# Layer 0's residual and norm steps held in PSUM, and convolution work moved from VectorE to GpSimd, in a two-layer hybrid trunk

## The chip, the cores and the metric

The kernel runs on one core of one Trainium2 chip. The engines of a core work in parallel, each through its own queue in order: TensorE (PE, with its weight loads as PEld), VectorE (DVE), ScalarE (ACT), GpSimd (POOL) and SyncE (SP), which issues all of this kernel's transfers. The metric is the device time of one execution in microseconds, as a median over runs.

## The reference

The input `x` is 512 rows of 1024 float32 numbers. Two layers each compute `x <- x + RMSNorm_post(mixer(RMSNorm_pre(x)))`.

```python
def rms_norm(x, g):
    return x * lax.rsqrt(jnp.mean(x * x, axis=-1, keepdims=True) + EPS) * g

for i in range(DEPTH):
    h = rms_norm(x, pre_norm_g[i])
    y = even_mixer(h, ...) if i % 2 == 0 else odd_mixer(h, ...)
    x = x + rms_norm(y, post_norm_g[i])
```

Layer 0's mixer is block-sparse attention beside a causal pooling mixer, layer 1's is an S5 state-space layer beside a Conformer convolution module. What the change touches of layer 1 is the convolution with its layer norm, and the gate of the state-space branch:

```python
def conformer_conv(a, gl, dw, ln_g, ln_b, pw):
    g = a * jax.nn.sigmoid(gl)
    c = causal_depthwise_conv(g, dw)            # 31 taps per channel
    mu = jnp.mean(c, axis=-1, keepdims=True)
    var = jnp.mean(jnp.square(c - mu), axis=-1, keepdims=True)
    n = (c - mu) * lax.rsqrt(var + EPS) * ln_g + ln_b
    return jax.nn.silu(n) @ pw

ya, yb = jnp.split(y @ glu_w + glu_b, 2, axis=-1)
ssm_out = ya * jax.nn.sigmoid(yb) * jax.nn.silu(gc)
```

## The kernel before

All products are done three times over on halves of the operands: a float32 number is split into a rounded high part and the rest (`split`, L108, and the weight splits in `prefetch`, L158), and `mm3` (L102) adds high by high, high by low and low by high into one PSUM bank. ScalarE writes the high part of a weight block (`whi`), and GpSimd (in layer 0's input projections VectorE) subtracts it from the loaded `raw` to get `wlo`. `prefetch` works up to three blocks ahead of TensorE.

The kernel is written in a tile framework. Tiles are taken from pools with a fixed number of buffers for each tag, and a new tile waits for the last reader of the old one in its buffer. The order of the instructions in each engine's queue is not that of the text: a scheduler lays it out before the run, by the place of the instruction in the text (its priority) and by when a simulated timeline has its inputs ready. `issue_after` forces instructions behind a given one on its engine. The queue is fixed once the kernel is built: an engine whose next instruction waits does nothing else.

Layer 0's end (L927 to L956). There are four row blocks t of 128 rows, each with two halves q of 512 columns. For each (t, q), `out_mm` forms the output projection in a PSUM bank `z`; banks come from the pool `pz` (four banks) except that the first halves of t=0 and t=1 live in `ps` (two banks). ScalarE takes the sum of squares (`sumsq`, L309), VectorE multiplies by the gain into an SBUF tile `yg` (a `wt`). When both halves are there, `add_norm` (L912) takes the root (`root2`, `root`: one ScalarE square root and small VectorE steps on 128x1 numbers, L92 to L100), forms the residual sum in `xt` by two wide `scalar_tensor_tensor`s, takes its sums of squares and root, and forms the next layer's normed input `xn` by two more. `next_hT` (L903) transposes `xn` of the block before on TensorE and splits it into `hh` and `hl`. Layer 1's first projection, `sa`, starts with the columns of t=0 and t=1 (L954), in four banks of `pz`, while the last blocks are still being normed; in the same stretch GpSimd splits `sa`'s weights.

The convolution (L1076 to L1124). There are four channel blocks m. `conv_in` (L1078) forms the gated input `gp[m]` when its projection is done: block 0 out of `sa`, 1 out of `sb`, 2 and 3 out of `ab1`. Each tap is one VectorE `scalar_tensor_tensor` on 128x512, which adds into `acc` in PSUM (one bank). The last `NP[m]` taps of a block are done elsewhere (`ptap`, L1092): ScalarE scales the shifted input into `lt`, and GpSimd adds it to `pacc` (two buffers). VectorE adds `pacc` to `acc` right after its first tap, and its last tap writes the sum `ca[m]` to SBUF. `conv` is called after each of the 16 weight blocks of `sb`, `ab1`, `gd` and `gc`, for eight VectorE taps and three others each time.

After the taps, `ln_mean` (L1126) adds the first three `ca`, and TensorE sums over the channels by two matmuls with `ones`, one on that sum (L1131) and one on `ca[3]` (L1132). `ln_var` and `ln_out` follow. The gate of the state-space branch comes from two projections `gl0` and `gl1` of four banks each (L1232 to L1243), which share the four banks of `pz`; `gl1` is forced behind the second mean matmul (`issue_after(ln["mu"])`, L1234). For each half, ScalarE takes a sigmoid, and two VectorE steps form `ct` (L1241, L1242) before it is split.

Of the kernel before, what the change touches and what calls it, by code (L numbers as in the profile page):

```python
# [14 lines left out]
F32 = mybir.dt.float32  # L15
# [3 lines left out]
AF = mybir.ActivationFunctionType  # L19
# [4 lines left out]
MUL, ADD, SUB, MAX, MIN = ALU.mult, ALU.add, ALU.subtract, ALU.max, ALU.min  # L24

T, D = 512, 1024
# [12 lines left out]
def tile_hybrid_trunk(ctx, tc, A):  # L39
# [17 lines left out]
    def tt(e, o, a, b, op):  # L57
        return e.tensor_tensor(o, a, b, op=op)  # L58

    def stt(e, o, a, s, b, op0, op1):  # L60
        e.scalar_tensor_tensor(o, a, s, b, op0=op0, op1=op1)  # L61
# [30 lines left out]
    def root(v, bias, n=1):  # L92

        q, w, r = (sm.tile([128, n], F32, tag=f"{a}{n}", name=a) for a in ("rq", "rw", "rr"))
        S.activation(q, v, AF.Sqrt, bias=bias)
        ts(V, w, v, bias, -0.5, ADD, MUL)
        V.reciprocal(r, q)
        stt(V, q, r, w, r, MUL, MUL)
        stt(V, r, q, 1.5, r, ADD, MUL)
        return r  # L100

    def mm3(p, sh, sl, mh, ml, start, stop):  # L102
# [206 lines left out]
    def sumsq(src, jpool):  # L309
        ss = sm.tile([128, 1], F32, tag="ss", name="ss")  # L310
        jk = jpool.tile([128, 512], BF16, tag="junk", name="junk", bufs=1)
        S.activation(jk[:, 0:src.shape[-1]], src, AF.Square, scale=1.0 / 32.0, accum_out=ss)  # L312
        return ss
# [16 lines left out]
    def wt():  # L330
        return wk.tile([128, 512], F32, tag="t", name="wt", bufs=5)
# [580 lines left out]
    def add_norm(t, yg, ss):  # L912

        r = root2(ss)
        ss = []
        for q in range(2):
            stt(V, xt[t][q], yg[q], r, xt[t][q], MUL, ADD)
            ss.append(sumsq(xt[t][q], wk))
        r = root2(ss)
        if t == 3:  # L920
            S.activation(warm, r, AF.Sigmoid)
        xn = [wt(), wt()]
        for q in range(2):
            stt(V, xn[q], xt[t][q], r, gpre1[q], MUL, MUL)
        return xn

    xns, yg, ss = [], defaultdict(list), defaultdict(list)  # L927
# [8 lines left out]
    for t, q in ((0, 0), (1, 0), (0, 1), (1, 1), (2, 0), (2, 1), (3, 0), (3, 1)):  # L936
        if t < 2 and not q:
            z = z2[t]
        else:
            z = pz.tile([128, 512], F32, tag="z", name="z")  # L940
            out_mm(z, f"o0{q}", full, t, ch, cl, OK0, lambda j: 3 - j)
        ss[t].append(sumsq(z, wk))
        yg[t].append(wt())
        tt(V, yg[t][q], z, gpost[q], MUL)
        if (t, q) == (3, 0):
            prefetch(index["sa", 0] + 4)
        if q:
            if t:
                next_hT(t - 1, xns[t - 1])
            xns.append(add_norm(t, yg[t], ss[t]))  # L950
# [133 lines left out]

    NP = (0, 0, 4, 12)
    taps = [(m, k) for m in range(4) for k in range(KC - NP[m])]
    ptaps = [(m, k) for m in range(4) for k in range(KC - NP[m], KC)]
    acc, pacc = {}, {}  # L1090
# [12 lines left out]
    def conv(n, n_p=3):  # L1103
        for _ in range(n_p):
            if ptaps and gp[ptaps[0][0]] is not None:
                ptap()
        for _ in range(min(n, len(taps))):
            m, k = taps[0]
            if gp[m] is None:
                return  # L1110
            taps.pop(0)
            src, c = gp[m][:, k:k + T], dw[:, m, k:k + 1]
            if k == 0:
                while any(i == m for i, _ in ptaps):
                    ptap()
                acc[m] = pa.tile([128, T], F32, tag="acc", name="acc")
                ts(V, acc[m], src, c, None, MUL)
                if NP[m]:
                    tt(V, acc[m], acc[m], pacc[m], ADD)
                continue  # L1120
            o = acc[m]
            if k == KC - NP[m] - 1:
                o = ca[m] = kp.tile([128, T], F32, tag="ca", name="ca", bufs=4)
            stt(V, o, src, c, acc[m], MUL, ADD)  # L1124

    def ln_mean():  # L1126
        s = lt()
        tt(V, s, ca[0], ca[1], ADD)
        tt(V, s, s, ca[2], ADD)
        mu = ps.tile([128, 512], F32, tag="s", name="mu")  # L1130
        nc.tensor.matmul(mu, ones, s, start=True, stop=False)  # L1131
        ln["mu"] = nc.tensor.matmul(mu, ones, ca[3], start=False, stop=True).ins  # L1132
        for m in range(4):
            tt(V, ca[m], ca[m], mu, SUB)

        def sq(m):
            q = lt()
            S.activation(q, ca[m], AF.Square)
            return q
        a, b, c, ln["q"] = (sq(m) for m in range(4))  # L1140
        tt(V, a, a, b, ADD)
        tt(V, a, a, c, ADD)
        ln["s"] = a
# [88 lines left out]
    for n in range(2):  # L1232

        with tc.issue_after(ln["mu"]) if n else nullcontext():  # L1234
            z = proj_c(f"gl{n}", yh, yl, nk=4)
        for i in range(2):
            m = 2 * n + i
            s = ct()
            S.activation(s, z[2 + i], AF.Sigmoid, bias=gb[:, 4 + m:5 + m])
            a = ct()  # L1240
            stt(V, a, z[i], gb[:, m:m + 1], s, ADD, MUL)  # L1241
            tt(V, a, a, sgc[:, m], MUL)  # L1242
            split(c1[0][:, m], c1[1][:, m], a)  # L1243
    ln_silu()
    c2 = (hp.tile([128, 4, T], F32R, tag="hh", name="c2h"), hp.tile([128, 4, T], F32R, tag="hl", name="c2l"))
# [81 lines left out]
```

## Time and profile before

| | us |
|---|---|
| median of 3 runs (lowest to highest) | 454.8 (451.93 to 456.48) |
| the profiled execution's own time | 454.7 |
| its span, first to last instruction | 452.9 |
| TensorE busy | 433.5 (96%) |
| VectorE busy | 339.3 (75%) |
| GpSimd busy | 250.9 (55%) |
| ScalarE busy | 245.3 (54%) |

All times of rows are counted from the start of the span. Matmuls overlap in the pipeline: one of 512 columns is shown as 0.39 us long, but the next starts 0.23 us after it, so pitches between starts are used and not lengths. `x12` in a timeline row means that so many instructions in a row are merged. The clock column (PEclk) is TensorE's granted clock as a share of full speed.

### The profile page before, as it was taken

Reading aid. Unit: us, or ns where it says so; the run is one execution under the profiler, and the core shown is the slowest. Engines: PE = TensorE matmul, PEld = TensorE weight load, DVE = VectorE, ACT = ScalarE, POOL = GpSimd, SP = SyncE. Lnnn points to the kernel's source line nnn. Section 1 sums busy time; section 2 is a strip of 40 time slices with the busy share of each in tenths; the row PEclk is TensorE's granted clock in tenths of the full one; section 3 lists DMA queues with packets and bytes.
Section 4 is the critical chain, followed back from the end, with each engine's and each line's share of the span. In section 5 each row is a group of like instructions: output and inputs, shape, how many; then the busy total and the mean of one; then the engine's idle time right before and its main releaser. Section 6 shows DMA issues by size and latency. Waiting matters only on the chain.

```text
span 452.9 us, 6747 instructions
## 1 busy us (share of the span) xinstructions
PE 433.5 (96%) x2185; PEld 360.9 (80%) x2185; DVE 339.3 (75%) x725; ACT 245.3 (54%) x453; POOL 250.9 (55%) x403
## 2 busy tenths in 40 slices
PE   6999999999999999899989999999999978999994
PEld 5788888888888887688889888878888756888884
DVE  3899996757887995328881979999899787546444
ACT  7655536635847534625841636659873444373431
POOL 1019996019999974900930966769999830440000
PEclk9999999999999999999989999999999998999999
DMA  7965264241331349520337684774253521122022
GB/s 244 258 121 182 82 198 144 90 129 48 130 92 40 117 139 368 151 86 2 97 112 197 194 241 134 223 217 118 85 182 107 172 95 48 51 91 93 0 80 107
DMA packets 62403, 59.58 MB, mean 132 GB/s; under 512 B 20537, under 2 KB 43713, under 8 KB 62368
## 3 DMA queue, kind: packets, MB, share of 16 engines
q1 hardware_dynamic: 62368, 59.16, 43.4%
q8 instruction: 17, 0.28, 0.2%
q14 instruction: 18, 0.15, 0.1%
HBM read 50.62 MB, written 8.52 MB: 131 GB/s over the span
## 4 chain that ended last, share of the span: by engine, by line
PE 89%; DVE 3%; DMA 3%; issue 1%; ACT 1%; POOL 1%; SPq 0%; DVEq 0%; ACTq 0%; POOLq 0%
PE z L104 26%; PE z L106 25%; PE z L105 25%; PE s L1018 2%; DMA raw<-e_w_out 2%; PE tp L327 2%; POOL wlo L58 1%; PE tp L727 1%; PE tp L595 1%; PE y L1060 1%; DMA qk<-x 1%; PE tp L689 1%; DVE wt L61 1%; DVE ct L58 1%; PE y L1056 1%
## 5 line engine op out<-in xcount | busy, mean ns | idle before, releaser
L58 POOL TENSOR_TENSOR wlo<-raw,whi 128x1024 fp32r<-128x1024 f32 (+2 forms) x50 | 87.9, 1775 | 75.9 <-ACT whi L168 44.1
L106 PE MATMUL z<-hh,wlo 128*128 128x512 f32 (+1 forms) x288 | 106.6, 372 | 0.0
L104 PE MATMUL z<-hh,whi 128*128 128x512 f32 (+1 forms) x288 | 106.5, 374 | 0.0
L105 PE MATMUL z<-hl,whi 128*128 128x512 f32 (+1 forms) x288 | 106.4, 370 | 0.0
L61 DVE SCALAR_TENSOR_TENSOR acc<-gp,dw,acc 128x512 f32<-128x512 f32 x100 | 75.0, 750 | 2.1
L104 PEld LDWEIGHTS z<-hh,whi 128*128 128x128 f32 x288 | 54.6, 191 | 9.3 <-issue 0.9
L106 PEld LDWEIGHTS z<-hh,wlo 128*128 128x128 f32 x288 | 55.0, 191 | 8.6
L105 PEld LDWEIGHTS z<-hl,whi 128*128 128x128 f32 x288 | 54.9, 191 | 8.7 <-issue 0.2
L168 ACT ACTIVATE whi<-raw 128x1024 fp32r<-128x1024 f32 x30 | 31.7, 1055 | 35.8 <-PE z L105 10.5
L58 POOL TENSOR_TENSOR tab<-tab,U 128x4 f32<-128x4 f32 (+6 forms) x112 | 42.3, 408 | 0.0
L61 DVE SCALAR_TENSOR_TENSOR wlo<-raw,gcol,whi 128x512 fp32r<-128x512 f32 x48 | 36.4, 781 | 6.6 <-ACT whi L173 4.8
L173 ACT ACTIVATE whi<-raw,gcol 128x512 fp32r<-128x512 f32 x48 | 32.1, 714 | 15.7 <-PE z L106 10.2
L104 PE MATMUL z<-whi,hh 128*128 128x512 f32 x96 | 37.6, 400 | 0.7 <-ACT whi L173 0.7
L105 PE MATMUL z<-wlo,hh 128*128 128x512 f32 x96 | 38.1, 398 | 0.0
L106 PE MATMUL z<-whi,hl 128*128 128x512 f32 x96 | 37.7, 397 | 0.0
L312 ACT ACTIVATE junk<-z 128x512 bf16<-128x512 f32 (+1 forms) x17 | 9.7, 568 | 27.2 <-PE z L106 27.1
L58 POOL TENSOR_TENSOR tab<-tab 128x4 f32<-128x4 f32 (+6 forms) x56 | 23.4, 438 | 0.0
L104 PEld LDWEIGHTS z<-whi,hh 128*128 128x128 f32 x96 | 18.0, 190 | 4.6 <-ACT whi L173 1.1
L105 PEld LDWEIGHTS z<-wlo,hh 128*128 128x128 f32 x96 | 18.2, 190 | 3.7 <-DVE wlo L61 0.2
L106 PEld LDWEIGHTS z<-whi,hl 128*128 128x128 f32 x96 | 18.2, 189 | 3.5
L58 POOL TENSOR_TENSOR dm<-dm,ident 32x256 f32<-32x256 f32 x2 | 1.8, 923 | 29.6 <-DMA dm<-o_d 29.5
L58 DVE TENSOR_TENSOR hl<-tp,hh 128x512 fp32r<-128x512 f32 x16 | 10.6, 680 | 10.1 <-ACT hh L109 10.1
(326 smaller groups left out, 1013.4 us busy)
## 6 DMA issues: line engine op xcount, KB each, us to landing
raw<-e_w_in SPq DMA_DIRECT2D x15, 512.0 KB, 4.2
raw<-e_w_in SPq DMA_DIRECT2D x18, 256.0 KB, 3.1
raw<-e_w_out SPq DMA_DIRECT2D x8, 512.0 KB, 6.3
raw<-o_w_in SPq DMA_DIRECT2D x16, 256.0 KB, 3.0
rot<-td SPq DMA_DIRECT2D x16, 256.0 KB, 5.4
raw<-o_w_in SPq DMA_DIRECT2D x8, 512.0 KB, 4.0
raw<-o_w_out SPq DMA_DIRECT2D x8, 512.0 KB, 3.7
qk<-x SPq DMA_DIRECT2D x8, 256.0 KB, 4.7
```

The costliest lines, as they stand in the source:

```text
L58: return e.tensor_tensor(o, a, b, op=op)
L61: e.scalar_tensor_tensor(o, a, s, b, op0=op0, op1=op1)
L104: nc.tensor.matmul(p, sh, mh, start=start, stop=False)
L105: nc.tensor.matmul(p, sh, ml, start=False, stop=False)
L106: return nc.tensor.matmul(p, sl, mh, start=False, stop=stop)
L168: S.activation(hi, b.raw, AF.Copy)
L173: S.activation(hi[:, h], b.raw[:, h], AF.Copy, scale=gc)
L312: S.activation(jk[:, 0:src.shape[-1]], src, AF.Square, scale=1.0 / 32.0, accum_out=ss)
L327: nc.tensor.transpose(p[:, i], src[:, tcol(i)], ident)
L595: nc.tensor.matmul(p[:, i], ev[:, h + i], IC[:, c % 2 * 4 + h + i], start=True, stop=True)
L689: nc.tensor.transpose(p[:, h], qs[t][:, h], ident)
L1018: nc.tensor.matmul(both[h][:, i], sets[m][0][hf, i], Ut[m][hf, i], start=True, stop=True)
```

## The change

In layer 0, `yg` is no longer an SBUF tile: the gain multiply writes back into the PSUM bank `z`, the residual sum is formed there, its sums of squares are taken there, ScalarE copies the sum to `xt`, and the norm reads the bank. The banks of t=3 come from `ps`. A root of one column takes `tensor_scalar` with two per-partition scalars for its two last steps. In the convolution `NP` becomes (6, 4, 4, 12), ten more taps by ScalarE and GpSimd, and `pacc` is added after VectorE's last tap, which writes `ca`. The two partial sums of the mean go to GpSimd. The gate's first step writes back into its PSUM bank.

```diff
--- before.py
+++ after.py
@@ -95,8 +95,12 @@
         S.activation(q, v, AF.Sqrt, bias=bias)
         ts(V, w, v, bias, -0.5, ADD, MUL)
         V.reciprocal(r, q)
-        stt(V, q, r, w, r, MUL, MUL)
-        stt(V, r, q, 1.5, r, ADD, MUL)
+        if n == 1:
+            ts(V, q, r, w, r, MUL, MUL)
+            ts(V, r, q, 1.5, r, ADD, MUL)
+        else:
+            stt(V, q, r, w, r, MUL, MUL)
+            stt(V, r, q, 1.5, r, ADD, MUL)
         return r
 
     def mm3(p, sh, sl, mh, ml, start, stop):
@@ -914,14 +918,15 @@
         r = root2(ss)
         ss = []
         for q in range(2):
-            stt(V, xt[t][q], yg[q], r, xt[t][q], MUL, ADD)
-            ss.append(sumsq(xt[t][q], wk))
+            stt(V, yg[q], yg[q], r, xt[t][q], MUL, ADD)
+            ss.append(sumsq(yg[q], wk))
+            S.activation(xt[t][q], yg[q], AF.Copy)
         r = root2(ss)
         if t == 3:
             S.activation(warm, r, AF.Sigmoid)
         xn = [wt(), wt()]
         for q in range(2):
-            stt(V, xn[q], xt[t][q], r, gpre1[q], MUL, MUL)
+            stt(V, xn[q], yg[q], r, gpre1[q], MUL, MUL)
         return xn
 
     xns, yg, ss = [], defaultdict(list), defaultdict(list)
@@ -937,11 +942,11 @@
         if t < 2 and not q:
             z = z2[t]
         else:
-            z = pz.tile([128, 512], F32, tag="z", name="z")
+            z = (ps if t == 3 else pz).tile([128, 512], F32, tag="s" if t == 3 else "z", name="z")
             out_mm(z, f"o0{q}", full, t, ch, cl, OK0, lambda j: 3 - j)
         ss[t].append(sumsq(z, wk))
-        yg[t].append(wt())
-        tt(V, yg[t][q], z, gpost[q], MUL)
+        yg[t].append(z)
+        tt(V, z, z, gpost[q], MUL)
         if (t, q) == (3, 0):
             prefetch(index["sa", 0] + 4)
         if q:
@@ -1084,7 +1089,7 @@
 
 
 
-    NP = (0, 0, 4, 12)
+    NP = (6, 4, 4, 12)
     taps = [(m, k) for m in range(4) for k in range(KC - NP[m])]
     ptaps = [(m, k) for m in range(4) for k in range(KC - NP[m], KC)]
     acc, pacc = {}, {}
@@ -1111,22 +1116,20 @@
             taps.pop(0)
             src, c = gp[m][:, k:k + T], dw[:, m, k:k + 1]
             if k == 0:
+                acc[m] = pa.tile([128, T], F32, tag="acc", name="acc")
+                ts(V, acc[m], src, c, None, MUL)
+                continue
+            stt(V, acc[m], src, c, acc[m], MUL, ADD)
+            if k == KC - NP[m] - 1:
                 while any(i == m for i, _ in ptaps):
                     ptap()
-                acc[m] = pa.tile([128, T], F32, tag="acc", name="acc")
-                ts(V, acc[m], src, c, None, MUL)
-                if NP[m]:
-                    tt(V, acc[m], acc[m], pacc[m], ADD)
-                continue
-            o = acc[m]
-            if k == KC - NP[m] - 1:
-                o = ca[m] = kp.tile([128, T], F32, tag="ca", name="ca", bufs=4)
-            stt(V, o, src, c, acc[m], MUL, ADD)
+                ca[m] = kp.tile([128, T], F32, tag="ca", name="ca", bufs=4)
+                tt(V, ca[m], acc[m], pacc[m], ADD)
 
     def ln_mean():
         s = lt()
-        tt(V, s, ca[0], ca[1], ADD)
-        tt(V, s, s, ca[2], ADD)
+        tt(G, s, ca[0], ca[1], ADD)
+        tt(G, s, s, ca[2], ADD)
         mu = ps.tile([128, 512], F32, tag="s", name="mu")
         nc.tensor.matmul(mu, ones, s, start=True, stop=False)
         ln["mu"] = nc.tensor.matmul(mu, ones, ca[3], start=False, stop=True).ins
@@ -1238,8 +1241,8 @@
             s = ct()
             S.activation(s, z[2 + i], AF.Sigmoid, bias=gb[:, 4 + m:5 + m])
             a = ct()
-            stt(V, a, z[i], gb[:, m:m + 1], s, ADD, MUL)
-            tt(V, a, a, sgc[:, m], MUL)
+            stt(V, z[i], z[i], gb[:, m:m + 1], s, ADD, MUL)
+            tt(V, a, z[i], sgc[:, m], MUL)
             split(c1[0][:, m], c1[1][:, m], a)
     ln_silu()
     c2 = (hp.tile([128, 4, T], F32R, tag="hh", name="c2h"), hp.tile([128, 4, T], F32R, tag="hl", name="c2l"))
```

## Rows read from the trace of the kernel before

**Rows 1.** The page, part 1: busy us (share of span) xinstructions, by engine.

```profile
PE 433.5 (96%) x2185; PEld 360.9 (80%) x2185; DVE 339.3 (75%) x725; ACT 245.3 (54%) x453; POOL 250.9 (55%) x403
```

**Rows 2.** Windows: stretch, length, busy us by engine, PEclk, DMA share, GB/s.

```profile
215.00:240.00 25.00, 23.03 (x144) 20.86 (x143) 18.43 (x35) 16.45 (x37) 14.93 (x18) 0.93 0.42 120
240.00:366.00 126.00, 126.00 (x691) 105.07 (x690) 108.11 (x152) 72.96 (x108) 95.63 (x77) 1.00 0.58 167
366.00:380.00 14.00, 8.71 (x30) 6.09 (x29) 12.69 (x17) 7.21 (x10) 4.75 (x2) 0.88 0.22 76
```

**Rows 3.** Timeline, TensorE, 215 to 233: start, length, what [idle before].

```profile
218.12 1.04 PE L327 MATMUL tp<-ident,wt 128*128 128x128 f32 x8
...
226.16 0.28 PE L105 MATMUL z<-hl,whi 128*128 128x256 f32 x1
227.37 0.63 PE L327 MATMUL tp<-ident,wt 128*128 128x128 f32 x4 [0.92 <-DVE wt L61]
229.04 1.08 PE L327 MATMUL tp<-ident,wt 128*128 128x128 f32 x4 [1.05 <-DVE wt L61]
...
232.44 0.28 PE L106 MATMUL z<-hh,wlo 128*128 128x256 f32 x1
```

**Rows 4.** Timeline, VectorE, 215 to 236 us.

```profile
221.90 0.21 DVE L67 TENSOR_SCALAR rw<-ss,se 128x1 f32<-128x1 f32 x1 [1.70 <-ACT junk L312]
...
223.77 1.28 DVE L61 SCALAR_TENSOR_TENSOR rq<-rr,rw 128x1 f32<-128x1 f32 x1
...
225.91 2.98 DVE L61 SCALAR_TENSOR_TENSOR wt<-xh,rr,gain 128x512 f32<-128x512 f32 x2
...
230.32 0.22 DVE L61 SCALAR_TENSOR_TENSOR rq<-rr,rw 128x1 f32<-128x1 f32 x1
...
230.76 1.42 DVE L61 SCALAR_TENSOR_TENSOR xh<-wt,rr,xh 128x512 f32<-128x512 f32 x2
```

**Rows 5.** Timeline, GpSimd, 215 to 236 us.

```profile
215.38 12.97 POOL L58 TENSOR_TENSOR wlo<-raw,whi 128x256 fp32r<-128x256 f32 x12 [21.99 <-ACT whi L109]
```

**Rows 6.** Timeline, TensorE, 356 to 380 us.

```profile
357.04 1.02 PE L1131 MATMUL mu<-lt,ones 128*128 128x512 f32 x2
...
370.05 0.40 PE L106 MATMUL z<-yh,wlo 128*128 128x512 f32 x1
375.74 2.08 PE L1132 MATMUL mu<-ca,ones 128*128 128x512 f32 x2 [5.29 <-DVE ca L61]
...
379.25 0.39 PE L105 MATMUL z<-yl,whi 128*128 128x512 f32 x1
```

**Rows 7.** Groups by form, VectorE, 249 to 377: busy us, mean ns | idle.

```profile
L61 DVE SCALAR_TENSOR_TENSOR acc<-gp,dw,acc 128x512 f32<-128x512 f32 x100 | 75.0, 750 | 2.1
...
L58 DVE TENSOR_TENSOR acc<-acc,pacc 128x512 f32<-128x512 f32 x2 | 1.4, 695 | 2.7 <-POOL pacc L58 2.7
L58 DVE TENSOR_TENSOR lt<-ca 128x512 f32<-128x512 f32 x1 | 1.1, 1150 | 0.0
```

**Rows 8.** Timeline, VectorE, 270 to 376 us.

```profile
279.49 0.68 DVE L58 TENSOR_TENSOR gp<-z,gp 128x512 f32<-128x512 f32 x1
...
281.98 0.75 DVE L65 TENSOR_SCALAR acc<-gp,dw 128x512 f32<-128x512 f32 x1
...
372.47 2.55 DVE L58 TENSOR_TENSOR ct<-ct,sgc 128x512 f32<-128x512 f32 x1
```

**Rows 9.** Timeline, ScalarE, 369 to 372 us.

```profile
369.13 1.28 ACT L1239 ACT_TABLE_LOAD   x1 [1.44 <-PE z L106]
370.43 0.69 ACT L1239 ACTIVATE ct<-z,gb 128x512 f32<-128x512 f32 x1
```

**Rows 10.** Groups by line, GpSimd, 240 to 378 us.

```profile
L58 POOL TENSOR_TENSOR pacc<-pacc,lt 128x512 f32<-128x512 f32 x14 | 18.1, 1294 | 0.2
```

**Rows 11.** Windows, columns as in rows 2, 249 to 360 us.

```profile
249.00:308.00 59.00, 59.00 (x329) 48.77 (x328) 54.71 (x77) 34.43 (x54) 43.24 (x37) 1.00 0.71 205
308.00:360.00 52.00, 52.00 (x262) 42.36 (x263) 46.26 (x64) 36.51 (x52) 49.70 (x35) 1.00 0.42 123
```

## The prediction

> **What bounds the kernel now.** I read the page's busy times first, then the windows by stage, then the timelines of TensorE, VectorE and GpSimd around each stretch in which TensorE is not full. TensorE is busy 433.5 us of a span of 452.9 [rows 1], so the most that any edit can give back is its idle time and what the lowered clock after an idle stretch costs. The windows show where that is, in the part that the change touches [rows 2]: from 240 to 366 us TensorE is busy for all of 126 us at full clock; from 215 to 240 it lacks 2.0 us and its clock averages 0.93; from 366 to 380 it lacks 5.3 us at 0.88. These two places are the whole case; I call them stage A and stage B. The rest of the missing 19.4 us lies at the start, before 215 and at the end, where the edits have next to nothing.
>
> Stage A [rows 3]. TensorE runs half-width matmuls of `sa` at a pitch of 0.12 us up to 226.16, then waits twice for VectorE's `wt`, whose transposes start at 227.37 and 229.04. From the next due issue, 226.28, to 232.44, where the pitch is 0.12 again, are 6.16 us. In it lie eight transposes, which take 0.79 us undisturbed (218.12 to the next matmul at 218.91 in the same timeline), and 12 half-width matmuls, 1.44 us. The place costs 6.16 - 0.79 - 1.44 = 3.9 us: 2.0 idle, the rest at the lower of the two clock levels (1.2 GHz against 2.4).
>
> Who makes VectorE late [rows 4, 5]: GpSimd splits weights without a break from 215.38 to 228.35. In that stretch a `scalar_tensor_tensor` of one element a partition takes 1.28 us and a wide pair 2.98; when GpSimd has stopped, the same take 0.22 and 1.42. One set (two small ones, a wide pair) lasts from 223.77 to 228.89, 5.1 us; the same set lasts from 230.32 to 232.18, 1.9 us.
>
> Stage B [rows 6]. The last `gl0` matmul is issued at 370.05, the next is due at 370.28, and full pace is back at 379.25. Between lie the second mean matmul (0.86 us: the first one, at 357.04, and one matmul of 0.23 take the 1.08 us until 358.12) and four matmuls of 0.23. The place costs 8.97 - 0.86 - 0.92 = 7.2 us, of which 5.3 are a wait for VectorE's `ca`, the last convolution sum, and the rest is the lower clock.
>
> **Part 1: layer 0 in PSUM, and the small `scalar_tensor_tensor`s.** The wide operations on `yg` and the final norm now have one operand in PSUM. The accumulating taps have that form and take 0.75 us each as a mean of 100 [rows 7], while GpSimd is busy for 43.2 of 59 and 49.7 of 52 us beside them [rows 11]; so I take 0.75. Bounds: 0.71 (half of 1.42) and 1.5 (half of 2.98) [rows 4]. The two small steps of each root become `tensor_scalar`s; one of that kind, 128x1, ran at 221.90, inside GpSimd's run, and took 0.21 [rows 4, 5]. So a set shrinks from 5.1 to 1.9 us, and row block t=2 has two such sets ahead of its transposes (the first is alike, from 215.36): 6.4 us. Against that stand four new ScalarE copies of `xt` in the two late blocks, about 0.6 us each (estimate from the 0.69 of a ScalarE operation of that size [rows 9]); at worst two stand in the chain: 1.2. The inputs of the transposes come 5.2 us earlier, where 2.7 are needed (229.04 against 226.28). Stage A's 3.9 us go.
>
> The new wait here: the `sa` banks are now the ones in which t=2 lives until its last multiply reads it. That multiply's first half ended near 227.4 [rows 4] and comes to about 222.2; the first `sa` matmul is due some ten pitches of 0.12 before 226.16 [rows 3], at about 225.0, with 2.8 us to spare. If the set did not shrink, TensorE would wait there, with everything else of `sa` queued behind it.
>
> The Trainium skill (SBUF — State Buffer, Who interferes with whom) says that `tensor_scalar` can also enter a mode that takes the port pair shared with GpSimd, and then blocks fully. The row at 221.90 does not bear that out for one element a partition [rows 4]. By that rule the small steps would stay at 2.1 us a set, two sets would gain only 3.1 less 1.2, 0.8 us of stage A's idle time would be left, and the sum below would rise by 0.8 to 1.6.
>
> **Part 2: taps moved to ScalarE and GpSimd, sums added last.** VectorE's queue from 249 to 375.7 is what makes `ca` late. Block m=0 loses six taps of 0.75 and gains an add of 0.70 [rows 7]: -3.8. Block m=1: four taps less, one add more: -2.3. Blocks 2 and 3 keep their counts; their add moves from the front to the end, and with it goes VectorE's 2.7 us wait for `pacc` [rows 7]. The two partial sums of the mean leave: -1.15 and about as much again, -2.3 [rows 7]. Together 11.1 us; from it I take up to 2.0 because block 1 cannot start before its input, which VectorE made only at 279.49 to 280.2, while block 0 would end at 281.98 - 3.8 = 278.2 [rows 8]. Ahead of the last tap also stood a `ct` multiply of 2.55 us [rows 8]; it will now be behind it, and shorter. So VectorE is done with `ca` at 375.7 - 9.1 - 2.5 = 364 or so, 6 us before TensorE asks at 370.3.
>
> GpSimd's side: eight added adds (five for m=0, three for m=1) and two partial sums, at 1.29 us [rows 10], 12.9 us. In 249 to 308 it has 59 - 43.2 = 15.8 us free [rows 11], room for the eight (10.3). After 308 it has 2.3 us free, so the two sums (2.6) come after its queue, by about 360 to 362, still ahead of 364. Bounds for GpSimd's delay: 0 and 12.9. ScalarE's ten more scaled copies, 0.7 each, lie in stretches where it is idle half of the time; I cost them at nothing, and at up to 0.7 each if a weight split stands behind one.
>
> Stage B's 7.2 us go, but something else is late next. `gl1` reuses the banks of `gl0`'s results, and the first bank now stays in use until the `ct` multiply has read it. The chain is a table load from 369.13, the sigmoid from 370.43 for 0.69 [rows 9], then 0.75 and 0.70 [rows 7]: it ends at 372.6. TensorE would be there at 370.28 + 0.86 = 371.1, or at 370.3 if the mean's matmul was done earlier: a wait of 1.4 to 2.3 us, none if the compiler's order puts another bank first. Stage A's idle time cost double by the clock; so 0 to 4, and I take 2.1.
>
> **Sum.** Against the profiled execution (454.7 us, span 452.9, and close to the median of 454.8): 454.7 - 3.9 - 7.2 + 2.1 = 445.7 us. The small root steps at the end of the kernel run without GpSimd beside them, 0.2 either way: nothing.
>
> **Rivals.** First, stage B stays. What speaks for it: pieces of the 11.1 us hang on inputs, and GpSimd's third and fourth accumulators (two buffers) now wait until VectorE has read the first and second. Against: 6 us of slack. Only A is gained: 454.7 - 3.9 = 450.8.
>
> Second, stage A stays: the order of ScalarE's queue puts the new copies and weight splits ahead of the sums of squares, and the `sa` banks come free no earlier than 227.4. Then those ten half-width matmuls run after the wait, 1.2 us: 454.7 + 1.2 - 7.2 + 2.1 = 450.8 as well. Against: it needs 5 us of new delay on an engine that got 2.4 us of work.
>
> Third, on the other side: GpSimd becomes the bound. The first mean matmul stands in TensorE's queue in front of most of `gl0` (357.04 [rows 6]) and now waits for a GpSimd sum. If all of the 12.9 us fall behind GpSimd's full stretch, that sum ends at 360 + 12.9 = 373 and TensorE stands for 16 us, plus 2 of lowered clock: 454.7 - 3.9 - 7.2 + 18 = 461.6. It decides from a delay of about 9 us, where the 11.1 are used up. Against: the 15.8 us free. The Trainium skill (GPSIMD Engine Reference, Performance versus the Vector engine) speaks against such a move: it calls GpSimd the wrong engine for ordinary elementwise work, about half VectorE's speed. The rows agree, 1.29 against 0.75 [rows 7, 10], but that rule prices the work and not where it lies.
>
> **How the numbers follow.** Forecast 0.70, first rival 0.12, second 0.10, third 0.08. A measurement here tells about 1% (4.5 us) from no change. The forecast is on the faster side; of the first two rivals a third or so ends just below 450.2. So faster by over 1% 0.78, within 1% 0.14, slower by over 1% 0.08. Range: the low end is 443.6 (no bank wait) less 1.6 for the spread of runs (451.9 to 456.5), 442.0; the high end takes in 450.8 and as much, 452.4.
>
> **What would show it.** Right: no `tensor_scalar` of a root and no wide pair above 0.3 and 1.6 us beside GpSimd; the transposes of t=2 without a wait for VectorE; the mean's second matmul with an idle time under 1 us; a new wait of 1 to 2 us at the first `gl1` matmuls. Wrong: a wait of TensorE on GpSimd's `lt`, a wait at the first `sa` matmul, or `ca` still the releaser with over 3 us.

## The result, and the profile after

The changed kernel takes 448.58 us as a median of nine runs (447.41 to 450.34), against 454.56 for nine runs of the kernel before beside it: a ratio of 0.988 [0.985, 0.991] (in brackets the 95% interval), and by the medians 6.0 us less. The forecast was 9.0 less. The profiled execution took 450.0 us, with a span of 448.2.

Some names of the late stage, for the rows below: `rsy` and `rst` are the small steps of the layer norm's inverse root, `rb` its copy to all partitions by TensorE, `nh` and `nl` the high and low parts of the normed convolution, which `pw` multiplies; `c1h` and `c1l` are those of the gate's output, `c2h` that of the convolution branch, both for the last output projection; `y` is the output of the state-space layer and `xf` its states.

The page, part 1, of the kernel after (columns as in [rows 1]):

```profile
PE 432.8 (97%) x2185; PEld 359.7 (80%) x2185; DVE 332.8 (74%) x715; ACT 254.3 (57%) x471; POOL 261.2 (58%) x413
```

The windows of the stages, as in [rows 2]:

```profile
215.00:240.00 25.00, 25.00 (x175) 23.12 (x174) 15.64 (x39) 18.54 (x41) 13.91 (x22) 1.00 0.44 128
240.00:366.00 126.00, 125.33 (x666) 103.09 (x665) 105.36 (x146) 79.83 (x118) 106.43 (x83) 1.00 0.58 165
366.00:380.00 14.00, 14.00 (x60) 10.94 (x60) 8.35 (x13) 8.20 (x12) 4.84 (x2) 1.00 0.22 77
```

TensorE is full at full clock in both places where it was not. The waits of TensorE in the later part are new ones (engine, line, what it waited for, us in total, times, longest):

```profile
PE z L109 <- DVE nl L58: 1.6, 1, 1.6
PE rb L1160 <- DVE rsy L61: 1.5, 1, 1.5
...
PE z L108 <- ACT gp L1086: 0.7, 1, 0.7
```

Stage A. VectorE's timeline, the rows that answer to [rows 4], and then GpSimd's, to [rows 5]:

```profile
225.40 0.27 DVE L67 TENSOR_SCALAR rq<-rr,rw 128x1 f32<-128x1 f32 x1
225.70 0.21 DVE L67 TENSOR_SCALAR rr<-rq,rr 128x1 f32<-128x1 f32 x1
225.95 1.41 DVE L61 SCALAR_TENSOR_TENSOR wt<-z,rr,gain 128x512 f32<-128x512 f32 x2
```

```profile
215.52 11.65 POOL L58 TENSOR_TENSOR wlo<-raw,whi 128x256 fp32r<-128x256 f32 x12 [21.96 <-ACT whi L113]
```

A set beside GpSimd now lasts 1.96 us (225.40 to 227.36), where it lasted 5.1; the forecast was 1.9. GpSimd gains as well: 11.65 us for the twelve splits that took 12.97.

TensorE's timeline around the last convolution sum, to [rows 6], and VectorE's beside it:

```profile
368.81 0.39 PE L110 MATMUL z<-yh,wlo 128*128 128x512 f32 x1
369.04 1.02 PE L1135 MATMUL mu<-ca,ones 128*128 128x512 f32 x2
369.93 0.50 PE L108 MATMUL z<-yh,whi 128*128 128x512 f32 x1
```

```profile
363.16 0.69 DVE L58 TENSOR_TENSOR ca<-acc,pacc 128x512 f32<-128x512 f32 x1
369.91 0.76 DVE L61 SCALAR_TENSOR_TENSOR z<-z,gb,ct 128x512 f32<-128x512 f32 x1 [6.06 <-ACT ct L1242]
```

`ca` is ready at 363.85, 5.2 us before the mean's second matmul starts on it, and VectorE then idles for 6.06 us. The first `gl1` matmul, at 369.93, follows the mean's without a gap, so the wait for a bank that the forecast priced at 2.1 us did not come.

What came instead are two new waits in the norm behind the convolution. VectorE there, then GpSimd beside it, then TensorE, which waits twice:

```profile
384.05 2.36 DVE L58 TENSOR_TENSOR rst<-rsy 128x4 f32<-128x4 f32 x1
...
398.02 5.27 DVE L58 TENSOR_TENSOR nl<-ct,nh 128x512 fp32r<-128x512 f32 x2 [1.48 <-ACT nh L113]
```

```profile
384.00 2.40 POOL L58 TENSOR_TENSOR wlo<-raw,whi 128x1024 fp32r<-128x1024 f32 x1 [0.80 <-ACT whi L172]
...
397.55 5.19 POOL L58 TENSOR_TENSOR wlo<-raw,whi 128x1024 fp32r<-128x1024 f32 x2 [11.15 <-ACT whi L172]
```

```profile
388.57 0.65 PE L1160 MATMUL rb<-ident,rsy 128*128 128x128 f32 x4 [1.47 <-DVE rsy L61]
403.35 0.51 PE L109 MATMUL z<-nl,whi 128*128 128x512 f32 x1 [1.55 <-DVE nl L58]
```

In the kernel before, VectorE at the same two places:

```profile
390.67 0.16 DVE L58 TENSOR_TENSOR rst<-rsy 128x4 f32<-128x4 f32 x1
...
393.49 1.23 DVE L58 TENSOR_TENSOR rst<-rsy 128x4 f32<-128x4 f32 x1
...
403.85 1.29 DVE L58 TENSOR_TENSOR nl<-ct,nh 128x512 fp32r<-128x512 f32 x2 [0.53 <-ACT nh L109]
```

An operation on 128x4 numbers that takes 0.16 us elsewhere lasts 2.36, from the start of GpSimd's weight split to its end. The pair of `nl` took 1.29 in the kernel before and takes 5.27 here. Both operations have two inputs in SBUF. The kernel before had such a hold in the root too, 1.23 us at 393.49 beside a split from 392.29 to 394.69, but TensorE did not wait for it. The Trainium skill (SBUF — State Buffer, Who interferes with whom) says that a VectorE instruction with two SBUF inputs contends with a GpSimd instruction that reads SBUF, and that whoever issues first keeps the other out; these rows agree. Its other rule, that `tensor_scalar`, under conditions on its operands, can also take the port pair shared with GpSimd, does not show for one element a partition: 0.27 and 0.21 us at 225.40 and 225.70, beside GpSimd.

The other new cost lies at 287 to 344 us, where TensorE forms the four blocks of `y` between other matmuls. Its timeline at the first block and at the wait for `gp`:

```profile
287.79 0.43 PE L1065 MATMUL y<-xf,gout 128*64 128x128 f32 x2
288.15 0.50 PE L109 MATMUL z<-hl,whi 128*128 128x512 f32 x1
...
288.81 1.16 PE L1023 MATMUL s<-ug,pin 64*128 64x128 f32 x8
289.90 1.09 PE L1065 MATMUL y<-xf,gout 128*64 128x128 f32 x14
290.92 0.50 PE L108 MATMUL z<-hh,whi 128*128 128x512 f32 x1
...
303.29 0.50 PE L108 MATMUL z<-hh,whi 128*128 128x512 f32 x1 [0.67 <-ACT gp L1086]
```

In the kernel before, the 16 matmuls that form a block's `y` stood together:

```profile
291.85 1.09 PE L1060 MATMUL y<-xf,gout 128*64 128x128 f32 x16
```

Now 2 are issued, other work, then 14, in all four blocks. From the start of each piece to the next instruction, the 64 take 6.27 us, with the 0.67 of the `gp` wait in it, where they took 4.10: the splitting costs 1.5.

To follow such sums through every run, I measure four stretches by the starts of TensorE's instructions: (a) first `sa` matmul to first `sb`; (b) to first `gl0`; (c) to first `pw` (the first on `nh`); (d) to the first on `c2h`. In the kernel before, run 1 and run 7 the first mean matmul (0.86 us, [rows 6]) lies in (b), elsewhere in (c). What lies behind (d) is 39.3 to 39.5 us in all of them. The start of (a) lies between 222.1 and 225.2; it moves mostly with early waits of TensorE that come and go, for ScalarE's `whi` at about 7 us (0.7 to 1.7) and for its `ch` at about 182 (0 to 2.2).

| kernel | ratio to before [95%] | a | b | c | d | sum |
|---|---|---|---|---|---|---|
| before | 1 | 28.60 | 105.70 | 43.25 | 11.01 | 188.6 |
| after | 0.988 [0.985, 0.991] | 24.76 | 107.24 | 38.73 | 12.86 | 183.6 |
| 1 layer 0 alone | 0.995 [0.994, 0.997] | 24.76 | 106.38 | 44.09 | 11.01 | 186.2 |
| 2 convolution and gate alone | 0.998 [0.996, 1.000] | 27.12 | 107.94 | 38.73 | 12.84 | 186.6 |
| 3 late splits on VectorE | 0.982 [0.980, 0.985] | 24.76 | 108.21 | 37.05 | 11.01 | 181.0 |
| 4 old root | 0.990 [0.988, 0.992] | 24.76 | 107.08 | 38.74 | 12.84 | 183.4 |
| 5 half of the moved taps | 0.984 [0.982, 0.987] | 24.76 | 104.83 | 38.73 | 12.83 | 181.2 |
| 6 runs 3 and 5 together | 0.977 [0.975, 0.979] | 24.76 | 104.84 | 37.07 | 11.01 | 177.7 |
| 7 mean's sums on VectorE | 0.990 [0.988, 0.991] | 24.76 | 108.31 | 38.04 | 12.83 | 183.9 |
| 8 gate in SBUF | 0.986 [0.984, 0.988] | 24.77 | 108.00 | 38.38 | 11.01 | 182.2 |
| 9 no moved taps | 0.985 [0.982, 0.988] | 24.76 | 104.82 | 38.74 | 12.85 | 181.2 |
| 10 run 9, late splits on VectorE | 0.978 [0.975, 0.981] | 24.76 | 105.09 | 37.08 | 11.01 | 177.9 |
| 11 sums added first | 0.999 [0.996, 1.001] | 24.76 | 105.17 | 44.68 | 13.80 | 188.4 |
| 12 two edits and the mean | 0.980 [0.977, 0.983] | 24.76 | 104.82 | 38.38 | 11.00 | 179.0 |

The median of the kernel before on the chips of the twelve runs is 452.8 to 453.0 us. By its ratio, the changed kernel would take 447.5 there.

### The profile page after: what moved, and what is told of

Its sections match the earlier page's. It is cut to its first block, busy times and chain, and to the rows that moved or that the text cites. A ratio compares the mean times of both kernels' runs of the same rounds, so it can differ in the third digit from the quotient of the medians.

```text
span 448.2 us, 6759 instructions
## 1 busy us (share of the span) xinstructions
PE 432.8 (97%) x2185; PEld 359.7 (80%) x2185; DVE 332.8 (74%) x715; ACT 254.3 (57%) x471; POOL 261.2 (58%) x413
## 4 chain that ended last, share of the span: by engine, by line
PE 87%; DVE 4%; DMA 4%; ACT 2%; SPq 1%; issue 1%; DVEq 0%; ACTq 0%
PE z L110 25%; PE z L108 25%; PE z L109 25%; PE s L1023 2%; PE tp L331 2%; DMA xh<-x 1%; DMA gain<-pre_norm_g 1%; DVE nl L58 1%; PE y L1065 1%; DMA raw<-e_w_in 1%; PE tp L731 1%; PE tp L599 1%; PE tp L693 1%; DVE rst L58 1%; DVE c1l L58 1%
## 5 line engine op out<-in xcount | busy, mean ns | idle before, releaser
L58 POOL TENSOR_TENSOR wlo<-raw,whi 128x1024 fp32r<-128x1024 f32 (+2 forms) x50 | 86.6, 1753 | 68.4 <-ACT whi L172 38.2
L110 PE MATMUL z<-hh,wlo 128*128 128x512 f32 (+1 forms) x288 | 105.2, 370 | 0.0
L61 DVE SCALAR_TENSOR_TENSOR acc<-gp,dw,acc 128x512 f32<-128x512 f32 x94 | 70.7, 752 | 2.3
L316 ACT ACTIVATE junk<-z 128x512 bf16<-128x512 f32 (+1 forms) x25 | 14.6, 586 | 31.3 <-PE z L110 26.2
L58 POOL TENSOR_TENSOR pacc<-pacc,lt 128x512 f32<-128x512 f32 x22 | 28.5, 1296 | 0.4
L58 POOL TENSOR_TENSOR tab<-tab 128x4 f32<-128x4 f32 (+6 forms) x56 | 24.3, 456 | 0.0
```

What stands on the lines that cost most here:

```text
L110: return nc.tensor.matmul(p, sl, mh, start=False, stop=stop)
```

## The experiments

All are edits of the changed kernel, except runs 1 and 2, which are edits of the kernel before.

**1 and 2: the two halves of the change, each alone.** Run 1 has the hunks of layer 0 and of the root, run 2 those of the convolution, the mean and the gate.

> Only the layer 0 part (the banks and the small root steps) is applied to the kernel before. Theory: stage A's 3.9 us go and nothing else changes; TensorE still waits over 5 us for the last convolution sum in stage B; 454.6 - 3.9 = 450.7 us. Rival: what stage A gives back, stage B takes, because VectorE's convolution queue does not move; the wait for the sum grows to about 9 us and the time stays at 454 to 455.

> Only the convolution, mean and gate parts are applied to the kernel before. Theory: stage B's 7.2 us go, stage A's 3.9 stay, and three new losses stand against it: about 1.6 us each at the layer norm's transposes and at the normed low parts, and about 2.4 before gl0, where the eight-group state outputs are cut in two and one sa or ab1 result is late; so 454.6 - 7.2 + 5.6 = 453.0 us. Rival: the new losses belong to the two parts together (an earlier TensorE that meets an unmoved GpSimd); then the waits are not here and the time is 454.6 - 7.2 = 447.4.

Run 1 takes 451.1 us, by its ratio 2.1 less than before, and run 2 451.7, by its ratio 1.0 less. The waits of TensorE in run 1, and then in run 2:

```profile
PE mu L1137 <- DVE ca L61: 5.3, 1, 5.3
...
PE z L108 <- ACT us L1009: 0.4, 1, 0.4
```

```profile
PE tp L327 <- DVE wt L61: 2.0, 2, 1.1
PE z L105 <- DVE nl L58: 1.5, 1, 1.5
...
PE rb L1155 <- DVE rsy L61: 1.5, 1, 1.5
...
PE z L104 <- ACT gp L1081: 1.4, 1, 1.4
```

Each half removes its own stage and leaves the other: stretch (a) falls to 24.76 in run 1 and the wait for `ca` is gone in run 2. Run 1 shows that winning time in stage A does not lengthen the wait in stage B: it is 5.30 us as before. The likely reason is that the convolution's inputs come from TensorE and move with it. Run 1 loses 1.5 of its 3.8 us again: 0.7 in (b), with a wait of 0.4 for ScalarE's `us`, and 0.8 in (c), where eight matmuls behind the wait for `ca` run at the lower pace and not four (granted clock 0.78 from 363 to 377, against 0.88 in [rows 2]). Run 2 wins 4.5 in (c), has all the new costs of the changed kernel in (b), (c) and (d), and comes out near nothing; of the 2.0 us by which its sum is shorter, 1.5 lie in (a), which its edits do not touch. So the new costs belong to the convolution half.

**3: the late weight splits on VectorE.**

```diff
-    add_group("pw", A["o_pw"][0], K4, [(0, 512)], G)
-    add_group("o10", A["o_w_out"][0], (2, 3), [(0, 512)], G, j0=2)
+    add_group("pw", A["o_pw"][0], K4, [(0, 512)], V)
+    add_group("o10", A["o_w_out"][0], (2, 3), [(0, 512)], V, j0=2)
```

> The changed kernel with the four last weight splits of GpSimd (o_pw and the second half of o10) given to VectorE. Theory: the two new waits of TensorE (1.5 us for the layer norm's root, 1.6 for a normed low part) come from GpSimd's splits, beside which VectorE's operations with two SBUF inputs stand still; without them both waits go: 448.6 - 3.3 = 445.3 us. Rival: they come from the length of VectorE's own queue; with four more splits of 1.2 us, 4.9 in all, the waits grow to 3 us or more: 449 to 452.

444.5 us. VectorE's timeline where the collisions were:

```profile
380.67 1.23 DVE L58 TENSOR_TENSOR wlo<-raw,whi 128x1024 fp32r<-128x1024 f32 x1
...
382.81 0.17 DVE L58 TENSOR_TENSOR rst<-rsy 128x4 f32<-128x4 f32 x1
...
395.47 1.29 DVE L58 TENSOR_TENSOR nl<-ct,nh 128x512 fp32r<-128x512 f32 x2 [0.54 <-ACT nh L113]
```

The split itself takes 1.23 us here and 2.40 on GpSimd, and none of these steps is held up. Both waits are gone, stretch (c) falls by 1.68 and (d) by 1.85, 3.5 in all. For `nl` the theory holds. For `rb` a second thing moved with the edit. In TensorE's queue the first part of the last output projection, 24 matmuls on `c1`, stands around `rb`: in the changed kernel, and in every run with the wait, `rb` comes after 18 of them, in the kernel before and in run 3 after all 24:

```profile
388.24 0.60 PE L1160 MATMUL rb<-ident,rsy 128*128 128x128 f32 x4
```

Six matmuls at 0.23 are 1.4 us, about as much as the wait of 1.47. So the hold by GpSimd and the earlier place of `rb` make this wait together, and run 3 takes both away.

**4: the root's two small steps as `scalar_tensor_tensor` again.**

```diff
-        if n == 1:
-            ts(V, q, r, w, r, MUL, MUL)
-            ts(V, r, q, 1.5, r, ADD, MUL)
-        else:
-            stt(V, q, r, w, r, MUL, MUL)
-            stt(V, r, q, 1.5, r, ADD, MUL)
+        stt(V, q, r, w, r, MUL, MUL)
+        stt(V, r, q, 1.5, r, ADD, MUL)
```

> The changed kernel with the two small root steps as before (scalar_tensor_tensor in place of tensor_scalar). Theory: each root beside GpSimd's splits takes about 1.5 us more, the row block t=2 has two roots ahead of its transposes and about 1 us to spare, so TensorE waits 1 to 2 us there and its clock drops: 450 to 452 us. Rival: the wide operations in PSUM are enough, no wait comes back: 448.6.

448.3 us, and (a) is 24.76 all the same. The theory falls, the rival holds. VectorE in the set ahead of the transposes:

```profile
222.90 0.76 DVE L61 SCALAR_TENSOR_TENSOR rq<-rr,rw 128x1 f32<-128x1 f32 x1
...
224.18 0.31 DVE L61 SCALAR_TENSOR_TENSOR rr<-rq,rr 128x1 f32<-128x1 f32 x1
...
224.53 1.41 DVE L61 SCALAR_TENSOR_TENSOR wt<-z,rr,gain 128x512 f32<-128x512 f32 x2
```

The small steps are still held up: they last 0.76 and 0.31 us here and up to 1.21 (at 215.81), where the same two take 0.22 and 0.16 without GpSimd. The wide pairs are not. Two wide pairs at 1.41 in place of 2.98 give 3.1 us, and 2.7 were needed.

**5: half of the moved taps.** `NP = (3, 2, 4, 12)` in place of `(6, 4, 4, 12)`.

> The changed kernel with the first two blocks' share of taps on ScalarE and GpSimd halved: NP = (3, 2, 4, 12) in place of (6, 4, 4, 12). Theory: the extra GpSimd sums stand ahead of GpSimd's part of the scan, so the compiler's order splits each block's 16 y<-xf matmuls into 2 and 14 with other work between (1.5 us over the four blocks) and the block after waits for ScalarE's gp (0.7 us). With five sums fewer the 16 are together again and the wait is gone: 2.2 us less than the changed kernel, a ratio to before of about 0.983. VectorE gets five taps of 0.75 back, 3.8 us, out of an idle time of 6.1 ahead of the gate, so ca stays in time. Rival: the 2.4 us that the stretch lost are the load on the engines as such and not the order of the y matmuls, or ca comes late by what VectorE gets back; then the ratio stays at 0.988 or rises.

444.9 us; (b) is 104.83, which with the 0.86 of the mean's matmul is the 105.70 of the kernel before. The 16 matmuls stand together and no wait for `gp` is left. Behind `ca`, VectorE still idles 5.60 us: with 3.8 us of work more, `ca` stands only 0.5 us worse (4.7 us ahead of its matmul, not 5.2).

**6: runs 3 and 5 together.**

> Both cures together: the weight splits of pw and of the second half of o10 on VectorE, as in the third run, and NP = (3, 2, 4, 12). Theory: the two losses lie in different stretches (285 to 305 and 380 to 405 us) and add: the 3.3 us of the third run and the 2.2 of the fewer taps, plus the 1 us by which that run's gp wait was longer than the changed kernel's, a ratio to before of about 0.975. Rival: TensorE ahead of 360 us comes earlier by what is won there, and VectorE, with five taps more, then makes ca late, so that the ratio stays near the third run's 0.982.

442.8 us, a ratio of 0.977 where 0.975 was expected: the two gains add. TensorE's timeline shows the `y` matmuls of a block in one piece:

```profile
287.55 1.09 PE L1065 MATMUL y<-xf,gout 128*64 128x128 f32 x16
```

**7 and 8: the mean's sums back on VectorE (`tt(V, ...)` for `tt(G, ...)` in `ln_mean`), and the gate's first step back in SBUF (the last hunk undone).**

> The changed kernel with the mean's two partial sums back on VectorE. Theory: VectorE has 6.1 us of idle time behind ca and the two sums cost it 1.4 to 2.3, so this part of the change is worth nothing by itself: the ratio to before stays at 0.988, and ca is still made some 4 us before TensorE asks. Rival: the part does carry the gain in stage B, and the wait for ca comes back with 1 us or more (0.991 or above).

> The changed kernel with the gate's first step writing a tile in SBUF again and not its PSUM bank. Theory: the gain in stage B comes from ca being early, and the bank wait that the PSUM form might cost did not come; the gate's second step has two SBUF inputs again and takes 2.4 us where a GpSimd split runs beside it, but nothing that TensorE asks for hangs on the first of them. The ratio to before stays at 0.988, within 0.3%. Rival: the PSUM form carries a part of the gain, because a gate step of 2.4 us stands ahead of the steps from the mean to the norm: 1 to 2 us more, 0.991 or above.

Run 7 takes 448.2 us, and no wait for `ca` comes back, as the theory says. But the two sums cost VectorE 4.5 us and not 1.4 to 2.3, and `ca` is ready only 0.8 us before its matmul, not the 4 that I had expected:

```profile
347.22 3.36 DVE L58 TENSOR_TENSOR lt<-ca 128x512 f32<-128x512 f32 x1
...
351.16 1.13 DVE L58 TENSOR_TENSOR lt<-lt,ca 128x512 f32<-128x512 f32 x1
...
368.45 0.76 DVE L61 SCALAR_TENSOR_TENSOR z<-z,gb,ct 128x512 f32<-128x512 f32 x1 [1.69 <-ACT ct L1242]
```

Run 8, 446.5 us, is inside the bound that I gave, but both readings missed what happened: (d) is back at 11.01. With the gate in SBUF the order laid out for the late stage is another, and neither `rsy` nor `nl` is waited for. `nl` no longer stands beside a split. The root still does:

```profile
383.62 2.25 DVE L61 SCALAR_TENSOR_TENSOR rsy<-rst,rsy 128x4 f32<-128x4 f32 x1
```

That step takes 0.16 us otherwise, but here `rb` comes after all 24 `c1` matmuls in TensorE's queue, and the root is ready 0.5 us ahead of it. A wait of 1.0 us for a `ct` is new at 386.58, ahead of `rb`. The gate's PSUM form gained nothing and in this order cost 2.2 us in (c) and (d).

**9, 10 and 11: is it the taps or the place of the sum?** Run 9 has `NP = (0, 0, 4, 12)` as before, with the sums of blocks 2 and 3 last:

```diff
-            stt(V, acc[m], src, c, acc[m], MUL, ADD)
-            if k == KC - NP[m] - 1:
+            o = acc[m]
+            if k == KC - 1:
+                o = ca[m] = kp.tile([128, T], F32, tag="ca", name="ca", bufs=4)
+            stt(V, o, src, c, acc[m], MUL, ADD)
+            if NP[m] and k == KC - NP[m] - 1:
```

Run 10 is run 9 with the edit of run 3. Run 11 has the `conv` of the kernel before, with the sum behind the first tap.

> The changed kernel with none of the added taps: NP = (0, 0, 4, 12) as before, but the sums of blocks 2 and 3 still added last, the mean on GpSimd and the gate in PSUM. Theory: VectorE's idle time behind ca was 5.6 us with half of the moved taps (fifth run); five taps of 0.75 more and two adds of 0.7 fewer leave about 3.2, so the moved taps were not needed for stage B, and the y<-xf matmuls stay together: ratio to before 0.984 as in the fifth run. Rival: the moved taps carry the gain, by the prediction's count 6.1 of its 11.1 us, and without them the wait for ca comes back with 2 us or more: 0.988 or above.

> The kernel of the run before this one with the weight splits of pw and of the second half of o10 on VectorE. Theory: as the sixth run, 0.977, since rb and nl are no longer waited for and the y matmuls stay together; at best a little less, with fewer sums on GpSimd. Rival: VectorE, with all taps of blocks 0 and 1 and four more splits, makes ca late: 0.982 or above.

> The changed kernel with the convolution as before: NP = (0, 0, 4, 12) and the sum of GpSimd added first; what is left of that part is the mean's partial sums on GpSimd and the gate in PSUM. Theory: the order of the sum is what makes ca early, because VectorE otherwise waits for pacc at the head of a block with all its other taps behind it (2.7 us in the kernel before) and for the longest at the last block, whose twelve taps GpSimd sums only at the end; the wait for ca comes back with 1 to 4 us, 0.987 or above. Rival: the two sums of the mean were most of the lateness (they took VectorE 4.5 us in the seventh run), ca comes just in time and the ratio is 0.984.

446.3, 443.1 and 452.5 us. VectorE in run 9, and then in run 11, at the last block:

```profile
345.25 14.21 DVE L61 SCALAR_TENSOR_TENSOR acc<-gp,dw,acc 128x512 f32<-128x512 f32 x18
359.57 0.69 DVE L58 TENSOR_TENSOR ca<-acc,pacc 128x512 f32<-128x512 f32 x1
365.26 0.76 DVE L61 SCALAR_TENSOR_TENSOR z<-z,gb,ct 128x512 f32<-128x512 f32 x1 [4.99 <-ACT ct L1245]
```

```profile
352.41 0.70 DVE L58 TENSOR_TENSOR acc<-acc,pacc 128x512 f32<-128x512 f32 x1 [6.28 <-POOL pacc L58]
353.15 10.25 DVE L61 SCALAR_TENSOR_TENSOR acc<-gp,dw,acc 128x512 f32<-128x512 f32 x13
365.71 0.76 DVE L61 SCALAR_TENSOR_TENSOR z<-z,gb,ct 128x512 f32<-128x512 f32 x1 [2.31 <-ACT ct L1244]
...
371.59 0.75 DVE L61 SCALAR_TENSOR_TENSOR ca<-gp,dw,acc 128x512 f32<-128x512 f32 x1
```

The two kernels differ only in the place of the sum. Added last, the 18 taps run without a break, GpSimd finishes `pacc` meanwhile, and `ca` is ready 4.1 us before its matmul without any moved tap. Added first, VectorE stands for 6.28 us with 18 taps queued behind the add, and TensorE waits 7.4 us for `ca`, more than the 1 to 4 that I had expected. So, with the mean on GpSimd, the place of the sum decides.

The stall is longer than the 2.7 us of the kernel before [rows 7] for two reasons of the same size. Counted from the first `gl0` matmul, VectorE is free for the add 1.8 us earlier, and `pacc` is done 1.8 us later; the mean's two sums, 2.6 us, now stand in GpSimd's queue ahead of `pacc`'s last add.

Nor is the stall all of the wait. In run 11 five steps of the gate stand among the last five taps, behind 2.31 us of waiting for a `ct`: from the end of the 13 taps at 363.40 to `ca` at 372.34 are 8.9 us, where five taps take 3.9 at the pitch of run 9's 18 (0.79). That is 5.0 us. In the kernel before, where two gate steps (one of them the `ct` of 2.55 in [rows 8]) and this wait stand among the last two taps, it is 3.8, counted in the same way from 370.32 to 375.68:

```profile
357.69 12.63 DVE L61 SCALAR_TENSOR_TENSOR acc<-gp,dw,acc 128x512 f32<-128x512 f32 x16
371.15 0.75 DVE L61 SCALAR_TENSOR_TENSOR ct<-z,gb,ct 128x512 f32<-128x512 f32 x1 [0.83 <-ACT ct L1239]
```

In run 9 the gate's steps come behind `ca`. Whether it is enough to put them there and leave the sum first was not tried.

**12: what seems to be enough.** Run 9 with the gate in SBUF and the old root: layer 0 in PSUM, the sum added last, the mean on GpSimd.

> What seems to be enough: the kernel before with layer 0 in PSUM, the sums of blocks 2 and 3 added last and the mean's partial sums on GpSimd; no moved taps, the gate in SBUF and the root's steps as before. Theory: stage A goes by the PSUM operands of the wide steps alone (fourth run), stage B by the place of the sum (ninth and eleventh), the y matmuls stay together without the moved taps, and with the gate in SBUF the splits fall beside other work than rsy and nl, as in the eighth run (2.5 us less between the first gl0 and the first c2h matmul than with the gate in PSUM): ratio to before 0.979, no wait over 0.5 us at ca, rsy or nl. Rival: the waits for rsy and nl come back in this order too, and the ratio is the 0.985 of the ninth run.

442.9 us, about what the theory says (0.980 for 0.979). The `rsy` step is held up as in run 8, 2.25 us at 380.24, and TensorE does not wait for it; its only wait behind 30 us is the one that run 8 had too:

```profile
PE z L104 <- DVE ct L61: 1.0, 1, 1.0
```

Runs 6, 10 and 12 beat both kernels, the kernel before by 0.020 to 0.023 of its time, and cannot be told apart by their intervals.

## Why the prediction was right, and where its terms were off

**Stage A, 3.9 us: right in size, one reason too many.** Stretch (a) falls by 3.84, there is no wait of the transposes and none at the first `sa` matmul, and the set has the length forecast. Of the two reasons given, the PSUM operands of the wide steps carry it alone; the `tensor_scalar`s are worth nothing that shows (run 4). The price itself holds a part that not every execution pays: in run 2 the two waits are as long as before, 2.0 us, but the granted clock from 215 to 240 was 1.00 and not 0.93 [rows 2], and (a) cost only 2.4 more than 24.76.

**Stage B, 7.2 us: right in size, wrong in its account.** Stretch (c) fell by 4.5; without the 0.86 of the mean's matmul that moved into it and the 1.7 of the new wait for `rb`, that is 7.1. `ca` was ready 5.2 us before its matmul, where 6 were forecast; that the clock times agree too, 363.85 and about 364, is chance, since TensorE comes to `gl0` 2.1 us earlier than before. But the sum behind that number fell short in two terms and was not needed in another. "With it goes VectorE's 2.7 us wait for `pacc`" counted the stall as it stood; with the mean's sums on GpSimd it is 6.28 (run 11). Of the gate's steps among the last taps the prediction counted 2.5 us for one `ct`; they cost 3.8 in the kernel before and 5.0 in run 11. The 6.1 us of moved taps are not needed at all (run 9). The mean's sums were taken at 2.3 and cost 4.5 in run 7, of which the first, held up beside GpSimd, took 3.36.

**The bank wait, +2.1: did not come.** The low bound, 0, was the value. The condition named for it, that the laid out order puts another bank first, is the likely cause, but the rows do not name the bank. Here the forecast had luck: this term stands against two that it lacked.

**Two terms were missing**, and they are why the gain was 5 to 6 us and not 9.0, or 11.1 without the bank wait.

The first is +3.5: `rb` and `nl` wait for VectorE operations with two SBUF inputs that stand beside GpSimd's weight splits, and `rb` besides comes six matmuls earlier in TensorE's queue (run 3 takes all of this away; which of the two would be enough for `rb` alone was not tried). The prediction saw this mechanism, since stage A is made of it, and a `ct` of 2.55 in [rows 8] too, but applied it only where the change removed it. Moving the late stage against GpSimd's splits put others of the same kind beside them.

The second is +2.4: (b) rose by 1.54, and without the 0.86 that moved out of it by 2.4, of which 1.5 are the divided `y` matmuls, 0.7 the wait for `gp` and the rest unassigned. The wait for `gp` is not one number: it is 0.5 to 1.6 us in the changed kernel and the five runs that keep all ten moved taps. "I cost them at nothing" stood for ScalarE's copies, and GpSimd's delay was priced only for the mean. With half of the moved taps both are gone (run 5). That the order changed is shown; why the scheduler divides the matmuls, presumably because GpSimd's part of their inputs comes later in its timeline, was only argued. Whether undivided matmuls with all sums kept would do as well was not tried.

The sum by these terms: -3.8 - 7.1 + 3.5 + 2.4 = -5.0, which is what the stretches say (188.6 to 183.6). The measured ratio gives 5.3 us [4.0, 6.7] and the two medians 6.0; the forecast was 9.0.

**The rivals.** Neither stage stayed, and no wait for `lt` appeared. Counted from the first `gl0` matmul, GpSimd's second sum was done 0.5 us after it, where VectorE's had been done 5.0 us before it: a delay of 5.5 us, short of the third rival's 9. The order laid out for TensorE also moved the first mean matmul, from 2.2 us ahead of `gl0` to 5.1 us into it; at its old place it would have waited 2.7 us for `lt`.

Whether the place of the sum would do without the mean on GpSimd was not tried. `ca` is 4.1 us ahead of its matmul in run 9 and 4.8 in run 12, and in run 7 the mean's sums cost 4.4 of such a lead, so it would be close.

## What to carry to other kernels

When an engine's queue has a fixed order, put the operation that joins another engine's result at the end of the chain, not at its head: everything behind it stands until that result is there. Freeing the engine earlier then lengthens the stall, and so does work added to the other engine's queue ahead of the result. Before work is moved between engines to remove a wait, see whether a change of place alone does it. And when a change moves a stage in time, look in the new place for operations with two SBUF inputs that end up beside GpSimd's long ones, and for what TensorE now asks for earlier; here it paid to move GpSimd's operations (run 3).

## What was unexpected of the hardware

A VectorE operation on 128x4 numbers was held for 2.36 us by one GpSimd subtraction of 2.40, 15 times its own length. The same weight split takes 1.23 us on VectorE and 2.40 on GpSimd, so moving it back cost VectorE half of what GpSimd had spent. And GpSimd's own run of twelve splits became 1.3 us shorter when VectorE's wide steps beside it read from PSUM: 11.65 us in the changed kernel and 11.66 in runs 1 and 4, against 12.95 in run 2, which leaves layer 0 as before.
